# Decoder block with expert mixer: digits in smaller groups, U chunks ahead of the one-hots, the last block's routes earlier, gate stores on ScalarE's queue

## The chip, the cores and the metric

The kernel runs on one core of one Trainium2 chip. The metric is the device time of one execution in microseconds, the median of several runs.

## What is computed

One decoder layer on 512 tokens of width 1024. Two groups of heads (16 state-space heads, 8 latent-attention heads) read one input projection and are mixed by one output projection. The change lies in what comes behind them, a product-key expert mixer (PEER): each token chooses, in each of 8 heads, 16 of 16384 experts.

```python
q = (xb @ w_query).reshape(T, PEER_HEADS, 2, PEER_HALF_DIM)
s = jnp.einsum('thkd,hknd->thkn', q, sub_keys).astype(jnp.float32)
sv, si = lax.top_k(s, K)                                   # K = 16 of 128, twice
cand_s = (sv[:, :, 0, :, None] + sv[:, :, 1, None, :]).reshape(T, PEER_HEADS, K * K)
cand_i = (si[:, :, 0, :, None] * PEER_N_KEYS + si[:, :, 1, None, :]).reshape(T, PEER_HEADS, K * K)
top_s, top_pos = lax.top_k(cand_s, K)
expert_idx = jnp.take_along_axis(cand_i, top_pos, axis=-1)
gate = jax.nn.softmax(top_s, axis=-1)
u = jnp.take(u_table, expert_idx, axis=0)
act = jax.nn.gelu(jnp.einsum('td,thkd->thk', xb, u), approximate=False)
v = jnp.take(v_table, expert_idx, axis=0)
return jnp.einsum('thk,thkd->td', gate * act, v)
```

The two expert tables are 16384 x 1024 float32 each.

## The kernel before

**Two ways through the experts.** Most tokens go densely: the kernel streams both whole tables once, in 128 chunks of 128 experts. A *U chunk* multiplies 128 rows of the first table with 352 tokens and puts GELU of the product into a tile `act` (`u_halves`, `act` at L1260). A *V chunk* multiplies that, weighted with the gates, with 128 rows of the second table into six PSUM accumulators (L1425, L1426, L1429). The tokens of block 3, and 32 tokens of block 2, fetch their experts' rows instead, by an indirect DMA of GpSimd, and VectorE makes the dot products: the *dots* (`ug_dots`, L1071) for the 32, the *gather* (`gather`, L1484 fetch, L1495 and L1511 products) for block 3.

**A weight.** Products keep float32's precision by three matmuls with split operands (L74, L75 with a high part, L76 with a low one). Each 128x1024 weight tile is loaded raw by SP (`wir`, L93), rounded by ScalarE into HI (`wih` or `wihx`, L111), and VectorE subtracts to get LO (`wil`, L121). Three raw and three LO tiles exist; HI runs one tile ahead. All engines, and SP's queue of loads, go through their instructions in the order in which the program issues them.

**The stages around the change.**
1. While the queries are made, `stage1` takes the 16 best scores per half head; after each second one, `sums` adds the two lists into candidates `cand` (on GpSimd), and a second search takes the best 16 of these.
2. `stage2` calls `routes` for three blocks at once (`nb` = 3): softmax of the best scores (difference `dd` L989, exponential on ScalarE L1010, sum L1011), and the arithmetic on VectorE that turns positions into expert numbers (`ijg`). ScalarE copies the indices into half precision (`tif`, L1019).
3. `build_g` makes a dense gate matrix by one-hot matmuls: 48 steps of 8 tokens. For each, VectorE makes one-hots `oj` (L1160) and `gi` (L1163) from *digits* of the expert numbers (`dhi` L1132, `dlo` L1133, `dgl` with gates L1141), PE does 16 small matmuls (L1185), and ScalarE evicts them into a staging tile `stg` (L1187). The digits are made for 32 tokens at a time, just before the first of them is used, and the last group's gate part in two halves. Every fourth step SP stores the tile in two pieces, 128 KB and 1920 KB (L1191, L1192). From step 1 each step also has one of the 32 dots. U half chunks (`step_u`) are put between the steps, paced evenly to 104 half chunks at the end of the 48 steps.
4. The V phase: U and V chunks in turn, one *pair* at a time. Gate tiles `gt` are loaded by SP (`load_g`), VectorE multiplies them with `act` (L1392), ScalarE and VectorE split the product into `Ph` (L1409) and `Pl` (L1417).
5. Beside it, block 3 runs as a generator (`gather`), advanced after each pair by `pump` with a budget of microseconds: `part(0)` does heads 0 to 3 (load of scores from a scratch tensor `s3d` L1456, searches L948 to L957, `routes` with `nb` = 1); then rows are fetched and used, and after every second row the second part, `part(4)`, heads 4 to 7, moves on by one step. Once rows have begun, their number is paced over the rest of the chunks.

Of the kernel before, what the change touches and what calls it, by code (L numbers as in the profile page):

```python
# [13 lines left out]
F16 = mybir.dt.float16  # L14
# [3 lines left out]
AF = mybir.ActivationFunctionType  # L18
# [13 lines left out]
UG = 32  # L32
# [23 lines left out]
def tile_block(ctx: ExitStack, tc: tile.TileContext, I, out):  # L56
# [914 lines left out]
    def stage1(m):  # L971
        yield top16(rt, sc.pop(m)[:, 0:3], 128, TV4[:, :, m], TI4[:, :, m])
        if m % 2:
            CD[m // 2] = rt.tile([128, 3, 88], F32, name="cand", bufs=2)
            sums(G, CD[m // 2], TV4[:, :, m - 1], TV4[:, :, m])
        for h in sorted(CD):
            if 2 * h + 1 < m or m == 15:
                yield top16(rt, CD.pop(h), 88, TS4[:, :, h], PO4[:, :, h])

    def routes(pl, ts, po, ti_, nb, nh, dst, after=lambda i: None, room=None):  # L980
# [5 lines left out]
        sm_ = lambda nm, dt=F32: pl.tile([128, n], dt, name=nm)  # L986
        d = pl.tile([128, nb, nh, 16], F32, name="dd")
# [6 lines left out]
        ab = lambda e: abf[:, :, e]  # L994
        V.tensor_scalar(p3, pos, 3, None, op0=OP.logical_shift_right)
# [14 lines left out]
        A.activation(f4(d), f4(d), AF.Exp)  # L1010
# [6 lines left out]
        for i in sorted(range(nb), key=lambda z: z != 2):  # L1017
            for c in range(2):
                A.activation(ti[:, i, :, :, :, c].rearrange("p e h a -> p h e a"),  # L1019
                             ti_[:, i].rearrange("p (h e) a -> p h e a", e=2), AF.Copy)  # L1020
            eq = room if room is not None else pl.tile(sh, F16, name="eq")
            abv = abf[:, i].rearrange("p e (h k) -> p (e h) k", k=16)
            V.tensor_tensor(eq, abv[:, :, None, :].to_broadcast(sh), IA["t"][:, None].to_broadcast(sh), op=OP.is_equal)
            yield 0.15 + nh * 0.27
            eqv = eq.rearrange("p g a (k c) -> p (g a) k c", c=2)
            tv = ti[:, i].rearrange("p e h a c -> p (e h a) c")
            V.tensor_tensor(eqv, eqv, tv[:, :, None, :].to_broadcast([128, 32 * nh, 8, 2]), op=OP.mult)
            yield 0.15 + nh * 0.27
            for w in (8, 4, 2):
                V.tensor_tensor(eq[:, :, :w], eq[:, :, :w], eq[:, :, w:2 * w], op=OP.add)  # L1030
            e4 = eq.rearrange("p (e h) a k -> p e h a k", e=2)
            V.tensor_tensor(dst(i)[:, 0:2], e4[:, :, :, 0], e4[:, :, :, 1], op=OP.add)
            yield 0.6 + nh * 0.27
            after(i)
# [89 lines left out]
    def digits(b, q0):  # L1124
        jT, gT, dT = GT[b]
        n = 32
        hi = gb.tile([128, n, 16, 2], F16, name="dhi")
        lo = gb.tile([128, n, 8, 2], F16, name="dlo")
        gl = gb.tile([128, n, 2, 8, 2], F16, name="dgl")
        dv = lambda e, w: dT[:, e, q0 * 2:(q0 + n) * 2].rearrange("p (q c) -> p q c", c=2)[:, :, None, :].to_broadcast([128, n, w, 2])  # L1130
        io = lambda w: iotaE[:, None, 0:w, :].to_broadcast([128, n, w, 2])
        V.tensor_tensor(hi, io(16), dv(0, 16), op=OP.is_equal)  # L1132
        V.tensor_tensor(lo, io(8), dv(1, 8), op=OP.is_equal)  # L1133
        DG[0] = hi, lo, gl
        yield 1.2

    def gated(b, q0, s0, s1):
        gT = GT[b][1]
        hi, lo, gl = DG[0]
        n = s1 - s0  # L1140
        V.tensor_tensor(gl[:, s0:s1], lo[:, s0:s1, None].to_broadcast([128, n, 2, 8, 2]),  # L1141
                        gT[:, q0 + s0:q0 + s1, :, None, :].to_broadcast([128, n, 2, 8, 2]), op=OP.mult)

    def build_g():
        def hot(n):
            b, g = divmod(n, 16)
            jT = GT[b][0]
            if g % 8 == 0:
                for _ in digits(b, g * 4):
                    pass  # L1150
            if g % 8 == 0:
                gated(b, g * 4, 0, 16 if n == 40 and UG == 32 else 32)
            if n == 48 - UG // 8 and UG == 32:
                gated(b, 32, 16, 32)
            q0 = g % 8 * 4
            hi, lo, gl = DG[0]
# [11 lines left out]

        nxt = hot(0)
        dots, head = ug_dots(), ug_head()  # L1170
        u0 = un[0] * 2 - (half[0] is not None)
        for n in range(48):
# [16 lines left out]
            if g % 4 == 3:  # L1189
                qv = lambda z: z.rearrange("j (q i) t -> j q (i t)", i=4)  # L1190
                nc.sync.dma_start(gs0[:, :, b * 4 + g // 4].rearrange("q j x -> j q x"), qv(stg[:, 0:8]))  # L1191
                nc.sync.dma_start(gsp[:, :, b * 4 + g // 4].rearrange("q j x -> j q x"), qv(stg[:, 8:]))  # L1192
            if g == 12 and b < 2:
                g_head(b + 1)
            if n >= DOT0:
                next(dots, 0.0)
            if HEAD0 <= n < HEAD0 + 5:
                next(head, 0.0)
            while un[0] * 2 - (half[0] is not None) < u0 + (2 * (LEAD - RES) - u0) * (n + 1) / 48:
                if not step_u(LEAD - RES if len(aps) > 1 else KEEP):  # L1200
                    break
# [164 lines left out]
    def load_g(q):  # L1366
        if q < 32 and q not in gt:
            gt[q] = vst.tile([128, NT // 32, 4, 32], F32, name="gt", bufs=2)
            nc.sync.dma_start(gt[q].rearrange("p b i t -> p (b i t)"),
# [71 lines left out]
    def gather():  # L1441
# [12 lines left out]
        def part(h0):  # L1454
# [6 lines left out]
            yield 0.1  # L1461
            for m in range(0, 8, 2):
# [25 lines left out]
        for s in range(256):  # L1488
# [5 lines left out]
            if s < 128:  # L1494
                V.scalar_tensor_tensor(r, r, 1.0, x3, op0=OP.mult, op1=OP.mult, accum_out=hd[:, s:s + 1])  # L1495
                if other is not None and s % 2:
# [207 lines left out]
```

## Time and profile before

| | |
|---|---|
| median of 3 runs | 1638.58 us (1638.53 to 1643.16) |
| the profiled execution | 1647.61 us |
| its span | 1645.8 us |
| its mean granted PE clock | 0.986 |
| DMA, whole span | 404.41 MB, mean 246 GB/s |

The profile is one execution, with a start, a length and the idle time ahead for each instruction or group of equal ones. In `start us, us, engine line op out<-in [idle before <-releaser]` the bracket is the time that the engine stood before the instruction, and what ended that. Records of one engine overlap a little, so the distance from start to start is what an instruction costs in a row of them. A row by windows gives the busy time of each engine in a stretch, the clock that PE was granted, the share of time in which the 16 DMA engines moved something, and GB/s. PE, PEld, DVE, ACT, POOL and SP are TensorE's matmuls, its weight loads, VectorE, ScalarE, GpSimd and SyncE.

### The profile page before, as it was taken

How to read it: one execution, taken by the hardware profiler on the slowest of the kernel's cores; microseconds unless marked ns; L12 is line 12 of the kernel's file. 1: busy time of each engine (PE TensorE's matmuls, PEld its weight loads, DVE VectorE, ACT ScalarE, POOL GpSimd, SP SyncE). 2: the span in 40 equal slices, each digit the busy share in tenths (PEclk: the TensorE clock that was granted, in tenths of full speed). 3: DMA queues.
4: the chain of work that ended last, by engine and by line, in shares of the span. 5: the costliest groups of instructions: out<-in, count | busy, mean ns of one | idle time of the engine just before them, and what ended most of it. 6: DMA issues, size and time to landing. Idle time of an engine off the chain costs nothing.

```text
span 1645.8 us, 23832 instructions
## 1 busy us (share of the span) xinstructions
PE 1578.0 (96%) x8640; PEld 1385.0 (84%) x8640; DVE 1361.7 (83%) x2684; ACT 692.6 (42%) x1106; POOL 496.3 (30%) x373
## 2 busy tenths in 40 slices
PE   7999989999999989889898989999999999999997
PEld 5778877888888989889887889999999999888886
DVE  8979678847677689988387989888888989999978
ACT  5575456631433445445342233333333333333332
POOL 0000000000144213320003455655555555555400
PEclk9999999999999999999999999999999999999999
DMA  6242121364433459997757889999999999999963
GB/s 242 92 153 90 46 62 47 108 233 141 137 101 99 130 179 328 335 332 238 243 159 275 311 307 395 369 359 371 358 350 380 354 362 361 372 358 336 369 227 118
DMA packets 158459, 404.41 MB, mean 246 GB/s; under 512 B 13100, under 2 KB 67820, under 8 KB 158084
## 3 DMA queue, kind: packets, MB, share of 16 engines
q1 hardware_dynamic: 110644, 238.88, 42.8%
q0 software_dynamic: 45248, 162.68, 26.9%
q8 instruction: 68, 1.11, 0.3%
q10 hardware_dynamic: 2448, 1.31, 0.3%
q14 instruction: 51, 0.42, 0.1%
HBM read 369.19 MB, written 32.59 MB: 244 GB/s over the span
## 4 chain that ended last, share of the span: by engine, by line
PE 77%; DVE 11%; DMA 6%; issue 2%; ACT 2%; POOL 1%; SPq 0%; DVEq 0%; ACTq 0%; POOLq 0%
PE va L1425 9%; PE va L1426 9%; PE va L1429 9%; PE pu L74 8%; PE pu L76 8%; PE pu L75 8%; DMA wir<-ut 3%; PE pw L76 3%; PE pw L75 3%; PE pw L74 3%; PE pa L74 3%; PE pa L76 3%; PE pa L75 3%; DVE wil L121 2%; DMA s<-s3d 1%
## 5 line engine op out<-in xcount | busy, mean ns | idle before, releaser
L111 ACT ACTIVATE wih<-wir 128x1024 fp32r<-128x1024 f32 (+2 forms) x269 | 278.1, 1035 | 293.7 <-DMA wir<-v 119.1
L121 DVE TENSOR_TENSOR wil<-wir,wih 128x1024 fp32r<-128x1024 f32 (+1 forms) x253 | 300.9, 1190 | 76.8 <-ACT wih L111 42.1
L76 PE MATMUL pu<-XTH,wil 128*128 128x352 f32 x1008 | 328.5, 326 | 18.4 <-DVE wil L121 18.4
L74 PE MATMUL pu<-XTH,wih 128*128 128x352 f32 x904 | 297.0, 329 | 0.9 <-ACT act L1260 0.9
L75 PE MATMUL pu<-XTL,wih 128*128 128x352 f32 x904 | 293.1, 324 | 0.0
L1426 PE MATMUL va<-wil,Ph 128*128 128x512 f32 x726 | 282.9, 390 | 0.0
L1484 POOL DMA_INDIRECT row<-u,ix x128 | 184.9, 1444 | 269.1 <-DVE row L1495 126.0
L1484 POOL DMA_INDIRECT row<-v,ix x128 | 189.2, 1478 | 155.6 <-DVE ac L1511 131.5
L76 PEld LDWEIGHTS pu<-XTH,wil 128*128 128x128 f32 x1008 | 192.2, 191 | 20.4 <-DVE wil L121 20.4
L74 PEld LDWEIGHTS pu<-XTH,wih 128*128 128x128 f32 x904 | 171.7, 190 | 4.1 <-ACT act L1260 1.2
L75 PEld LDWEIGHTS pu<-XTL,wih 128*128 128x128 f32 x904 | 171.8, 190 | 2.9
L1425 PE MATMUL va<-wih,Ph 128*128 128x512 f32 x432 | 168.3, 390 | 0.0
L1511 DVE SCALAR_TENSOR_TENSOR ac<-row,hd,ac 128x1024 f32<-128x1024 f32 x128 | 164.1, 1282 | 3.9 <-DMA row<-v,ix 1.7
L1495 DVE SCALAR_TENSOR_TENSOR row<-row,x 128x1024 f32<-128x1024 f32 x128 | 151.9, 1219 | 11.5 <-DMA row<-u,ix 10.2
L1426 PEld LDWEIGHTS va<-wil,Ph 128*128 128x128 f32 x726 | 136.3, 188 | 25.8
L111 ACT ACTIVATE wihx<-wir 128x1024 fp32r<-128x1024 f32 x67 | 71.0, 1060 | 193.4 <-DMA wir<-v 164.4
L1429 PE MATMUL va<-wih,Pl 128*128 128x512 f32 x432 | 133.0, 389 | 0.0
L1260 ACT ACTIVATE act<-pu 128x352 f32<-128x352 f32 x126 | 58.2, 462 | 146.5 <-PE pu L76 142.1
L1425 PE MATMUL va<-wihx,Ph 128*128 128x512 f32 x294 | 114.8, 390 | 0.8 <-ACT Ph L1409 0.8
L121 DVE TENSOR_TENSOR wil<-wir,wihx 128x1024 fp32r<-128x1024 f32 x62 | 75.8, 1222 | 33.9 <-issue 25.1
L1429 PEld LDWEIGHTS va<-wih,Pl 128*128 128x128 f32 x432 | 81.1, 188 | 17.0
L1425 PEld LDWEIGHTS va<-wih,Ph 128*128 128x128 f32 x432 | 81.1, 188 | 15.6
(469 smaller groups left out, 3023.3 us busy)
## 6 DMA issues: line engine op xcount, KB each, us to landing
wir<-ut SPq DMA_DIRECT2D x128, 512.0 KB
wir<-v SPq DMA_DIRECT2D x128, 512.0 KB
gsp<-stg SPq DMA_DIRECT2D x12, 1920.0 KB
gt<-gsp SPq DMA_DIRECT2D x30, 768.0 KB
wir<-wo SPq DMA_DIRECT2D x26, 512.0 KB
wir<-wf SPq DMA_DIRECT2D x18, 512.0 KB
wir<-wqr SPq DMA_DIRECT2D x16, 512.0 KB
de<-acd POOLq DMA_DIRECT2D x8, 512.0 KB
```

The costliest lines, as they stand in the source:

```text
L74: T.matmul(ps, lh, rh, start=start, stop=False)
L75: T.matmul(ps, lh, rl, start=False, stop=False)
L76: T.matmul(ps, ll, rh, start=False, stop=stop)
L111: A.activation(h, r, AF.Copy)
L121: self.lo(n).tensor_tensor(l, r, h, op=OP.subtract)
L1260: A.activation(ACT[c], ps, AF.Gelu)
L1425: T.matmul(va[b][e], Ph[b], h[:, cs], start=c == 0, stop=False)
L1426: T.matmul(va[b][e], Ph[b], l[:, cs], start=False, stop=False)
L1429: T.matmul(va[b][e], Pl[b], h[:, cs], start=False, stop=c == 127)
L1484: G.indirect_dma_start(out=R[s], out_offset=None, in_=I["u"] if s < 128 else I["v"], in_offset=bass.IndirectOffsetOnAxis(ap=ix[:, s % 128: ...
L1495: V.scalar_tensor_tensor(r, r, 1.0, x3, op0=OP.mult, op1=OP.mult, accum_out=hd[:, s:s + 1])
L1511: V.scalar_tensor_tensor(ac, r, hd[:, s - 128:s - 127], ac, op0=OP.mult, op1=OP.add)
```

## The change

It has eight parts.

1. In `stage1`, the last candidate sums (m = 15) move from GpSimd to VectorE.
2. In `routes` for one block (`nb` = 1), the exponential and the two index copies go to ScalarE right behind the difference `dd`, ahead of the position arithmetic. For three blocks nothing moves.
3. Digits are made for 16 tokens at a time, all three parts together, in double buffers, two steps ahead of their use.
4. Two U half chunks go between the first digits and the first one-hots, and one behind these; the pace under the 48 steps is steeper up to step 32 and flatter after.
5. The gate stores are issued by ScalarE.
6. The first two gate loads are issued by GpSimd.
7. Each part of the last block yields 9.0 us of budget between the load of its scores and the first search.
8. `part(4)` starts behind row 10 instead of row 0.

```diff
@@ stage1
-            sums(G, CD[m // 2], TV4[:, :, m - 1], TV4[:, :, m])
+            sums(V if m == 15 else G, CD[m // 2], TV4[:, :, m - 1], TV4[:, :, m])
@@ routes
+        def tis(i):
+            for c in range(2):
+                A.activation(ti[:, i, :, :, :, c].rearrange("p e h a -> p h e a"),
+                             ti_[:, i].rearrange("p (h e) a -> p h e a", e=2), AF.Copy)
...
+        if nb == 1:
+            A.activation(f4(d), f4(d), AF.Exp)
+            tis(0)
         V.tensor_scalar(p3, pos, 3, None, op0=OP.logical_shift_right)
...
-        A.activation(f4(d), f4(d), AF.Exp)
+        if nb > 1:
+            A.activation(f4(d), f4(d), AF.Exp)
...
-            for c in range(2):
-                A.activation(ti[:, i, :, :, :, c].rearrange("p e h a -> p h e a"),
-                             ti_[:, i].rearrange("p (h e) a -> p h e a", e=2), AF.Copy)
+            if nb > 1:
+                tis(i)
@@ digits
-    def digits(b, q0):
+    def digits(n):
+        b, g = divmod(n, 16)
         jT, gT, dT = GT[b]
-        n = 32
-        hi = gb.tile([128, n, 16, 2], F16, name="dhi")
+        q0, w = g * 4, 16
+        hi = gb.tile([128, w, 16, 2], F16, name="dhi", bufs=2)
...
@@ build_g, hot(n)
-            if g % 8 == 0:
-                for _ in digits(b, g * 4):
-                    pass
-            if g % 8 == 0:
-                gated(b, g * 4, 0, 16 if n == 40 and UG == 32 else 32)
-            if n == 48 - UG // 8 and UG == 32:
-                gated(b, 32, 16, 32)
-            q0 = g % 8 * 4
-            hi, lo, gl = DG[0]
+            hi, lo, gl = DG[n // 4 * 4]
+            if n % 4 == 3:
+                DG.pop(n - 3)
+            q0 = g % 4 * 4
@@ build_g
+        digits(0)
+        for _ in range(2):
+            step_u()
         nxt = hot(0)
+        step_u()
...
-                nc.sync.dma_start(gs0[:, :, b * 4 + g // 4].rearrange("q j x -> j q x"), qv(stg[:, 0:8]))
-                nc.sync.dma_start(gsp[:, :, b * 4 + g // 4].rearrange("q j x -> j q x"), qv(stg[:, 8:]))
+                nc.scalar.dma_start(gs0[:, :, b * 4 + g // 4].rearrange("q j x -> j q x"), qv(stg[:, 0:8]))
+                nc.scalar.dma_start(gsp[:, :, b * 4 + g // 4].rearrange("q j x -> j q x"), qv(stg[:, 8:]))
...
+            if n % 4 == 2 and n < 44:
+                digits(n + 2)
...
-            while un[0] * 2 - (half[0] is not None) < u0 + (2 * (LEAD - RES) - u0) * (n + 1) / 48:
+            um = 2 * (KEEP - 1)
+            to = u0 + (um - u0) * (n + 1) / 32 if n < 32 else um + (2 * (LEAD - RES) - um) * (n - 31) / 16
+            while un[0] * 2 - (half[0] is not None) < to:
@@ load_g
-            nc.sync.dma_start(gt[q].rearrange("p b i t -> p (b i t)"),
+            (G if q < 2 else nc.sync).dma_start(gt[q].rearrange("p b i t -> p (b i t)"),
@@ gather, part(h0)
             yield 0.1
+            yield 9.0
             for m in range(0, 8, 2):
@@ gather, rows
-                if other is not None and s % 2:
+                if other is not None and s > 10 and s % 2:
```

The first place is VectorE at the start of the 48 steps. Before, behind the last routes:

```order
L1032 TENSOR_TENSOR ijg<-eq 128x256
L121 TENSOR_TENSOR wil<-wir,wih 128x1024
L1132 TENSOR_TENSOR dhi<-iotaE,dT 128x1024
L1133 TENSOR_TENSOR dlo<-iotaE,dT 128x512
L1141 TENSOR_TENSOR dgl<-dlo,gT 128x1024
L1160 TENSOR_TENSOR oj<-iotaE,jT 128x1024
L1163 TENSOR_TENSOR gi<-dhi,dgl 128x2048
L1160 TENSOR_TENSOR oj<-iotaE,jT 128x1024
L1163 TENSOR_TENSOR gi<-dhi,dgl 128x2048
L121 TENSOR_TENSOR wil<-wir,wih 128x1024
```

And now, the same engine and place:

```order
L1041 TENSOR_TENSOR ijg<-eq 128x256
L121 TENSOR_TENSOR wil<-wir,wih 128x1024
L1142 TENSOR_TENSOR dhi<-iotaE,dT 128x512
L1143 TENSOR_TENSOR dlo<-iotaE,dT 128x256
L1144 TENSOR_TENSOR dgl<-dlo,gT 128x512
L121 TENSOR_TENSOR wil<-wir,wih 128x1024
L1159 TENSOR_TENSOR oj<-iotaE,jT 128x1024
L1162 TENSOR_TENSOR gi<-dhi,dgl 128x2048
L121 TENSOR_TENSOR wil<-wir,wih 128x1024
L1159 TENSOR_TENSOR oj<-iotaE,jT 128x1024
L1162 TENSOR_TENSOR gi<-dhi,dgl 128x2048
```

The digits have half the elements, and a LO subtraction for a U half chunk stands before each of the first two pairs of one-hots, where both pairs stood together.

The second place is the stores. Before, on SP, between the loads of weights:

```order
L93 DMA wir<-ut 128x1024 x14
L1191 DMA gs_69<-stg 128x2x128
L1192 DMA gsp<-stg 128x30x128
L93 DMA wir<-ut 128x1024 x2
L1191 DMA gs_69<-stg 128x2x128
L1192 DMA gsp<-stg 128x30x128
```

Now they stand on ScalarE, between evictions and HI copies:

```order
L1267 ACTIVATE act<-pu 128x352
L1190 ACTIVATE stg<-pw 128x128x4 x2
L1194 DMA gs_69<-stg 128x2x128
L1195 DMA gsp<-stg 128x30x128
L111 ACTIVATE wih<-wir 128x1024
```

SP has nothing left but loads there, and ScalarE issues each pair of stores right behind the eviction that fills the tile.

The third place is VectorE where the second part of the last block's routes begins beside the gathered rows. Before:

```order
L121 TENSOR_TENSOR wil<-wir,wih 128x1024
L1495 SCALAR_TENSOR_TENSOR row,hd<-row,x_8496 128x1024 x2
L948 MAX tv_9078<-s_9076 128x8 x2
L950 MAX_INDEX ti_9079<-tv_9078,s_9076 128x8 x2
L953 MATCH_REPLACE t_9154<-tv_9078,s_9076 128x128
```

Now:

```order
L121 TENSOR_TENSOR wil<-wir,wih 128x1024
L1503 SCALAR_TENSOR_TENSOR row,hd<-row,x_8531 128x1024 x4
L121 TENSOR_TENSOR wil<-wir,wih 128x1024
L1424 TENSOR_TENSOR Pl<-gt,Ph 128x384
L1399 TENSOR_TENSOR gt<-act,gt 128x11x32
L121 TENSOR_TENSOR wil<-wir,wihx 128x1024
L1503 SCALAR_TENSOR_TENSOR row,hd<-row,x_8531 128x1024
L948 MAX tv_9581<-s_9579 128x8 x2
L950 MAX_INDEX ti_9582<-tv_9581,s_9579 128x8 x2
```

The first search (MAX) of the second part comes behind 16 rows of the gather now, where it came behind four.

More of the change, by code (lines that the diff above doesn't have):

```diff
@@ L1122, in tile_block @@
     DG = {}
-    def digits(b, q0):
+    def digits(n):
+        b, g = divmod(n, 16)
         jT, gT, dT = GT[b]
-        n = 32
-        hi = gb.tile([128, n, 16, 2], F16, name="dhi")
[L1128 to L1131, printed above, removed]
+        q0, w = g * 4, 16
+        hi = gb.tile([128, w, 16, 2], F16, name="dhi", bufs=2)
+        lo = gb.tile([128, w, 8, 2], F16, name="dlo", bufs=2)
+        gl = gb.tile([128, w, 2, 8, 2], F16, name="dgl", bufs=2)
+        dv = lambda e, k: dT[:, e, q0 * 2:(q0 + w) * 2].rearrange("p (q c) -> p q c", c=2)[:, :, None, :].to_broadcast([128, w, k, 2])
+        io = lambda k: iotaE[:, None, 0:k, :].to_broadcast([128, w, k, 2])
         V.tensor_tensor(hi, io(16), dv(0, 16), op=OP.is_equal)
         V.tensor_tensor(lo, io(8), dv(1, 8), op=OP.is_equal)
[L1134 to L1138, printed above, removed]
-        hi, lo, gl = DG[0]
-        n = s1 - s0
-        V.tensor_tensor(gl[:, s0:s1], lo[:, s0:s1, None].to_broadcast([128, n, 2, 8, 2]),
-                        gT[:, q0 + s0:q0 + s1, :, None, :].to_broadcast([128, n, 2, 8, 2]), op=OP.mult)
+        V.tensor_tensor(gl, lo[:, :, None].to_broadcast([128, w, 2, 8, 2]),
+                        gT[:, q0:q0 + w, :, None, :].to_broadcast([128, w, 2, 8, 2]), op=OP.mult)
+        DG[n] = hi, lo, gl
     def build_g():
@@ L1147, in hot @@
             jT = GT[b][0]
-            if g % 8 == 0:
-                for _ in digits(b, g * 4):
-                    pass
-            if g % 8 == 0:
-                gated(b, g * 4, 0, 16 if n == 40 and UG == 32 else 32)
-            if n == 48 - UG // 8 and UG == 32:
-                gated(b, 32, 16, 32)
-            q0 = g % 8 * 4
-            hi, lo, gl = DG[0]
+            hi, lo, gl = DG[n // 4 * 4]
+            if n % 4 == 3:
+                DG.pop(n - 3)
+            q0 = g % 4 * 4
             oj = gb.tile([128, 4, 128, 2], F16, name="oj", bufs=2)
```

## The prediction

> **What bounds the kernel now.** I read the page first. TensorE (PE) sets the time.
>
> ```profile
> PE 1578.0 (96%) x8640; PEld 1385.0 (84%) x8640; DVE 1361.7 (83%) x2684; ACT 692.6 (42%) x1106; POOL 496.3 (30%) x373
> ```
>
> A change can win only where PE stands still or runs at a low clock, so the waits of PE come next, then the busy times by stretch: one row for the 48 steps of one-hots and dots, one for their middle, one for the start of the V phase, one for the last block's second half of scores and routes, one for the steady pairs of a U and a V chunk, and one for 20 of those.
>
> ```profile
> PE pu L76 <- DVE wil L121: 18.4, 7, 6.9
> PE pw L1185 <- DVE gi L1163: 13.9, 8, 4.3
> ```
>
> ```profile
> 603.35:741.60 138.25, 127.54 (x1095) 121.89 (x1093) 128.44 (x172) 68.97 (x124) 41.12 (x29) 0.97 0.94 313
> 620.00:720.00 100.00, 91.94 (x815) 87.50 (x813) 95.06 (x127) 49.70 (x87) 36.10 (x25) 1.00 1.01 342
> 820.00:840.00 20.00, 14.61 (x70) 13.68 (x71) 18.22 (x73) 5.51 (x8) 0.00 (x0) 0.83 0.54 171
> 878.65:975.91 97.26, 85.79 (x425) 76.66 (x424) 84.64 (x220) 32.49 (x45) 40.31 (x30) 0.95 0.83 295
> 960.00:1300.00 340.00, 339.08 (x1786) 309.01 (x1787) 302.75 (x419) 125.06 (x171) 193.86 (x133) 0.99 0.97 362
> 980.00:1000.00 20.00, 20.00 (x110) 18.32 (x109) 18.61 (x29) 5.77 (x8) 12.88 (x9) 1.00 0.99 388
> ```
>
> The columns are stretch, length, busy PE, PEld, DVE (VectorE), ACT (ScalarE), POOL (GpSimd), granted clock, DMA share and GB/s. In the steady pairs PE is busy 339.08 of 340 us: nothing is to be had there. In the dots VectorE is the fuller engine (128.44 against 127.54), in their middle clearly (95.06 against 91.94), with the DMA engines at 1.01. At the start of the V phase PE is busy 14.61 of 20 at clock 0.83, with VectorE at 18.22. In the second half of the routes PE has 85.79 of 97.26. Call these places A, B and C; the change works on all three.
>
> **A: one-hots and dots.** Before the 48 steps VectorE makes digits for 32 tokens and two one-hots, and PE waits for them.
>
> ```profile
> 601.75 1.86 PE L1185 MATMUL pw<-gi,oj 128*128 128x128 f16 x16 [4.30 <-DVE gi L1163]
> ...
> 609.06 0.32 PE L76 MATMUL pu<-XTH,wil 128*128 128x352 f32 x1
> 609.22 1.10 PE L1185 MATMUL pw<-gi,oj 128*128 128x128 f16 x16
> ```
>
> ```profile
> 598.21 0.68 DVE L1132 TENSOR_TENSOR dhi<-iotaE,dT 128x1024 f16<-128x1024 f16 x1
> 598.81 0.42 DVE L1133 TENSOR_TENSOR dlo<-iotaE,dT 128x512 f16<-128x512 f16 x1
> 599.26 0.69 DVE L1141 TENSOR_TENSOR dgl<-dlo,gT 128x1024 f16<-128x1024 f16 x1
> 599.87 0.69 DVE L1160 TENSOR_TENSOR oj<-iotaE,jT 128x1024 f16<-128x1024 f16 x1
> 600.48 1.22 DVE L1163 TENSOR_TENSOR gi<-dhi,dgl 128x2048 f16<-128x2048 f16 x1
> 601.61 0.69 DVE L1160 TENSOR_TENSOR oj<-iotaE,jT 128x1024 f16<-128x1024 f16 x1
> 602.21 1.22 DVE L1163 TENSOR_TENSOR gi<-dhi,dgl 128x2048 f16<-128x2048 f16 x1
> 603.35 1.22 DVE L121 TENSOR_TENSOR wil<-wir,wih 128x1024 fp32r<-128x1024 f32 x1
> ```
>
> After the wait the same 16 matmuls take 1.86 us instead of 1.10, so the gap costs a slow clock as well. By the starts, digits for 32 tokens take 1.66 us (598.21 to 599.87), an oj 0.61, a gi 1.13 (600.48 to 601.61). The changed kernel has half-size digits; between half and all of 1.66 I estimate 1.1. It puts three U half chunks on PE before the first one-hot matmuls. A half chunk is 12 matmuls, and one starts 0.16 us after the other (609.06 to 609.22), so it takes 1.92 us. Three are 5.76 us, more than the 4.30 that PE waits. The order puts two LO subtractions between the digits and the second pair of one-hots, each at the 1.13 of a gi, whose record is as long; VectorE then starts its steady part at 598.21 + 1.1 + 2 x 1.13 + 2 x 1.74 = 605.05, against 603.35. From there to 741.6 it has 128.44 us of work and 9.8 idle. After: one LO fewer (-1.1), eight digit groups of 1.1 instead of four of 1.66 (+2.2): 129.6. With half of the idle time kept, 4.5, it ends at 739.2, 2.4 earlier, and one whole U chunk (3.84 us of PE) further. **A = -6.2.** Bounds: if all idle time stays, 605.05 + 129.6 + 9.8 = 744.5, which with the chunk gives -1; if none stays, 734.7 and -10.8. "U thicker" is hardly done under the dots themselves: by the order a step there has 1.41 half chunks, and 1.42 before; what counts is the three ahead.
>
> The last candidate sums on VectorE end this wait, the earlier start is 10.8 us less about 0.5 for three sums:
>
> ```profile
> 549.12 0.56 DVE L948 MAX8 ts<-cand 128x8 f32<-128x88 f32 x3 [10.80 <-POOL cand L965]
> ...
> 563.29 0.55 DVE L1011 TENSOR_REDUCE smm<-dd 128x24 f32<-128x384 f32 x1 [3.69 <-ACT dd L1010]
> ```
>
> I cost it at nothing. The exponential of that stage (three blocks, not moved by the change) keeps its place in ScalarE's row behind the U evictions that PE paces, and VectorE already waits 3.69 us for it at 563.29: what it gains at 549 it waits there. If that is wrong, up to 10 us more are to be had, which would show as VectorE reaching the digits before 590.
>
> The stores by ScalarE: SP issued one in 0.46 us, so 24 of them put some 11 us on ScalarE, which has 69 us of idle time in 138.25. The cover is that idle time; what is gained is that the next weight loads do not queue behind a store that waits for its staging tile.
>
> ```profile
> 632.77 0.46 SPq L1192 DMA_DIRECT2D gsp<-stg  x1
> 636.36 6.11 SPq L93 DMA_DIRECT2D wir<-ut  x1
> ```
>
> That gain lies in the 5 us of idle that I take off A. The two first gate loads by GpSimd no longer stand behind SP's loads of weights. VectorE waited for them here:
>
> ```profile
> 804.71 0.53 DVE L1392 TENSOR_TENSOR gt<-act,gt 128x352 f32<-128x352 f32 x1 [6.01 <-DMA gt<-gs]
> ```
>
> PE still had U chunks to do, so I give it 0, between -1 and +1.
>
> **B: start of the V phase.** The load of the last block's scores was issued at 812.02, and VectorE, its next user in order, stood 8.76 us until 819.43; everything behind it, the LO of the next weights too, was late, and PE waited 6.93 us for that.
>
> ```profile
> 819.43 0.49 DVE L948 MAX8 tv<-s 128x8 f32<-128x128 f32 x2 [8.76 <-DMA s<-s3d]
> ```
>
> ```profile
> 812.02 0.43 SPq L1456 DMA_DIRECT2D s<-s3d  x1
> ```
>
> ```profile
> 825.39 0.66 PE L76 MATMUL pu<-XTH,wil 128*128 128x352 f32 x1 [6.93 <-DVE wil L121]
> ```
>
> ```profile
> 814.08 0.46 ACT L1260 ACTIVATE act<-pu 128x352 f32<-128x352 f32 x1
> ...
> 831.05 0.47 ACT L1260 ACTIVATE act<-pu 128x352 f32<-128x352 f32 x1
> ...
> 838.99 0.47 ACT L1260 ACTIVATE act<-pu 128x352 f32<-128x352 f32 x1 [2.73 <-PE pu L76]
> ```
>
> From eviction to eviction an undisturbed pair takes 7.94 us (831.05 to 838.99); the two from 814.08 to 838.99 took 24.91, so 9.0 were lost. The change lets the first search start two V chunks, some 16 us, after the load: twice the 7.4 that it took to land. Next late would be the search work itself, and VectorE's two LO tiles of lead cover a burst. **B = -9**, bounds -7 (its work shows at one pair) and -9.8 (with the clock kept up).
>
> **C: second half of the routes beside the gather.**
>
> ```profile
> L1260 ACT ACTIVATE act<-pu x11: 438/446/465, 878.7 to 975.9; 128x352 f32<-128x352 f32 x11
> ```
>
> Eleven evictions, so ten pairs, in 97.26 us: 17.9 over ten of 7.94. VectorE's row says of what: its 84.64 busy is 5.2 over 79.4, and 12.6 was idle. Most of that idle is two waits:
>
> ```profile
> 889.38 0.49 DVE L948 MAX8 tv<-s 128x8 f32<-128x128 f32 x2 [5.09 <-DMA s<-s3d]
> ...
> 955.61 0.22 DVE L1011 TENSOR_REDUCE smm<-dd 128x4 f32<-128x64 f32 x1 [5.19 <-ACT dd L1010]
> ```
>
> ```profile
> 952.54 1.06 ACT L111 ACTIVATE wih<-wir 128x1024 fp32r<-128x1024 f32 x1 [4.26 <-DMA wir<-ut]
> ```
>
> The exponential stood behind a HI copy that waited 4.26 us for its weights. After: the score load goes out four rows (more than a pair) before its use, and the exponential goes to ScalarE some ten VectorE operations and two rows earlier. The idle time goes, the 5.2 of work stays. **C = -12.6**; bounds -7.7 (only the two waits go, 10.3, and 2.6 come back as weights that are late) and -17.9 (the lead hides the work too).
>
> **Steady pairs.** By the order the gather starts three V chunks later and ends at the same chunk: 256 rows over some 79 pairs instead of 82, 3.24 a pair for 3.12, 0.06 MB on 2.87 (two weight loads, 3.12 rows of 0.524 MB, a quarter of a 768 KB gate load): 370 GB/s where 362 ran. The 388 at 980 passed with PE busy all 20 us. I take +1, bounds 0 and +6.
>
> **Sum:** -6.2 - 9 - 12.6 + 1 = -26.8 against the profiled execution's 1647.61, so 1620.8; that one lay 9.03 over the median of three, 1638.58, and I take the same difference off it: **1611.8**.
>
> **Rivals.** *The DMA engines set the pace.* Where PE falls behind they are at 1.01 with 342 GB/s, and a store issued by another engine moves the same bytes. Then A is only what leaves the full stretch early, three half chunks or 0.79 MB at 342 GB/s, -2.3; B and C stay (C's 28.7 MB at 362 GB/s fit in 79.3 us); and if 362 GB/s is the most that the steady mix gets, 2.2% of 79 pairs of 7.94 us come on top, +13.8. Sum -10, 1628. For it: the share of 0.97. Against: 388 GB/s at 980. The Trainium skill (DMA: Bandwidth & Descriptors, "Issuing engines are not separate DMA queues") says that transfers started by different engines run on the same 16 DMA engines and save only issue time, and its section "Where 436 GB/s comes from" puts a core's HBM at about 358 GB/s, which would give this rival's time; the trace's 362 over 340 us is near that figure and its 388 over 20 us above it, so the row decides for now.
>
> *Stores hold ScalarE up; slower.* Its row is in order: HI copies, evictions and GELU stand behind a store that takes long to issue. A single issue behind such a store took 6.11 us on SP. With HI one chunk ahead, 3.84 us are hidden; 12 times (6.11 - 3.84) is +27.2, which cancels all the gain: about 1639. At 8 us an issue it is +50, so 1662. It decides from 6.1 us an issue. Against it: SP's own 0.46 for the store itself.
>
> *All waits go:* A -10.8, B -9.8, C -17.9, together -38.5: 1600.
>
> **How the numbers follow.** Forecast 0.55, DMA pace 0.25, all waits 0.08, ScalarE held up 0.12 (a part of it small, 0.02 still faster, 0.05 at no change, 0.05 slower). The forecast's own range, is 1604 to 1620: the bounds lie some 5, 1.5, 5 and 3 us from the terms of A, B, C and the steady pairs, and errors of their own are together about 8. To hold 8 in 10 it must reach into the DMA case and the full gain: 1600 to 1631. About 0.3%, 4.9 us, is what a measurement of this kernel can tell from no change; the DMA case has a tenth of its chance there. Faster 0.55 + 0.22 + 0.08 + 0.02 = 0.87, same 0.08, slower 0.05.
>
> **What would show it.** Right: no wait of PE for gi over 1 us before the first one-hot matmuls; no wait of VectorE over 2 us for the scores at either search; evictions 7.94 us apart through the first ten pairs; the dots ending some 2 us earlier. Wrong: steady pairs over 8.0 us with the DMA share at 1 (the DMA rival); waits on ScalarE or of VectorE for wih behind each store (the ScalarE rival); VectorE's waits moved to weights instead of gone.

## The result

The changed kernel takes 1628.37 us (median of 4 runs, 1626.13 to 1628.64); the kernel before takes 1640.3 beside it and 1641.64 over 29 runs of the experiments' first series. The ratio to before is 0.9923, 95% interval 0.9903 to 0.9942: about 12 to 13 us faster, where 26.8 were forecast. The time lies in the range given, 16.6 us above the forecast of 1611.8.

The first two rows of the page after, and PE's longest waits:

```profile
span 1624.4 us, 23835 instructions
...
PE 1571.6 (97%) x8640; PEld 1379.0 (85%) x8640; DVE 1364.0 (84%) x2704; ACT 693.5 (43%) x1106; POOL 513.8 (32%) x372
```

```profile
PE pa L287 <- ACT XH L282: 11.5, 2, 10.9
PE pw L1188 <- DVE gi L1162: 8.2, 7, 2.1
PE pu L76 <- DVE wil L121: 7.6, 5, 4.2
```

PE's wait for LO fell from 18.4 to 7.6 us, that for the one-hots from 13.9 to 8.2. The wait for XH lies in the first stage, which the change does not touch.

Profile against profile the gain is 21.4 us (1645.8 to 1624.4), median against median 12 to 13. To see where both numbers come from I cut each trace at five instructions: the first eviction of a U chunk, the last one-hot matmul (`pw<-gi,oj`), and three of the low-part products of the V chunks (`va` from `Pl`, six a chunk): the first, the 49th (ninth chunk) and the 169th (twenty-ninth chunk). Starts are taken from the trace, differences in us. An undisturbed pair takes 7.93 us, so eight of them are 63.5 and twenty 158.7. What lies ahead of the first U eviction is left out of the table: no edit stands there, and it took from 529.9 to 533.2 us in these traces (533.2 in the first profile of before, 531.3 in the changed kernel).

| kernel | first U to last one-hot | to the first V product | 8 V chunks (B) | next 20 (C) | to the end |
|---|---|---|---|---|---|
| before, first profile | 258.2 | 15.5 | 72.5 | 175.7 | 590.7 |
| before, second profile | 258.3 | 15.3 | 72.2 | 169.2 | 590.7 |
| changed | 250.9 | 16.8 | 63.5 | 171.0 | 590.8 |
| only one-hots | 248.8 | 15.3 | 73.5 | 172.8 | 590.8 |
| only queues | 255.3 | 16.1 | 72.0 | 173.7 | 590.8 |
| only first gap | 257.5 | 15.4 | 63.5 | 170.4 | 590.8 |
| only second part | 256.8 | 15.4 | 72.3 | 167.9 | 590.7 |
| three ahead | 255.0 | 15.4 | 73.9 | 172.7 | 590.8 |
| all but queues | 251.7 | 15.6 | 63.5 | 171.1 | 590.7 |
| all but exponential | 251.0 | 16.3 | 63.5 | 171.8 | 591.1 |
| all, scores earlier | 249.9 | 16.4 | 63.5 | 167.1 | 590.8 |
| all, spread | 250.1 | 16.4 | 63.5 | 162.0 | 590.8 |
| all, rows thin | 250.0 | 16.4 | 63.5 | 160.0 | 610.1 |
| gap and spread | 257.6 | 15.6 | 63.5 | 163.4 | 590.7 |

Three columns decide. A (the first two) and B changed as forecast; C hardly changed, and C is also the only stretch of the table that two executions of one and the same program do not repeat (175.7 and 169.2).

Now the places. At the first one-hots of the changed kernel PE goes from a U matmul straight into the 16 small ones (the row holds the first 14 of them):

```profile
601.00 0.32 PE L76 MATMUL pu<-XTH,wil 128*128 128x352 f32 x1
601.17 0.99 PE L1188 MATMUL pw<-gi,oj 128*128 128x128 f16 x14
```

The windows of the changed kernel, in the columns of the prediction: the steps that have a dot, the first eight V chunks, the twenty behind them, a stretch at the second part's first search, and the steady pairs.

```profile
603.00:740.00 137.00, 128.50 (x1109) 122.31 (x1108) 133.65 (x191) 71.33 (x123) 40.09 (x30) 0.98 0.97 326
799.00:862.50 63.50, 63.50 (x338) 57.75 (x337) 45.60 (x151) 28.61 (x41) 0.00 (x0) 1.00 0.57 184
862.50:1033.50 171.00, 163.26 (x842) 146.88 (x841) 150.60 (x319) 59.81 (x83) 83.38 (x60) 0.98 0.88 318
930.00:950.00 20.00, 16.19 (x73) 15.15 (x74) 20.00 (x69) 5.66 (x9) 7.63 (x7) 0.83 0.76 257
1055.00:1380.00 325.00, 325.00 (x1722) 295.63 (x1721) 292.94 (x361) 120.41 (x166) 191.55 (x133) 1.00 0.99 375
```

The first eight V chunks are without a gap (63.50 of 63.50). In the steps with dots VectorE is at 133.65 of 137. (The prediction calls its row to 741.60 that of all 48 steps; the one-hot matmuls go on, to 791.4 before and 782.2 now.) At 930 the picture of the old B is back: PE at 16.19 of 20 and clock 0.83, VectorE full. What begins there, in the order VectorE, SP, PE:

```profile
925.57 0.49 DVE L948 MAX8 tv<-s 128x8 f32<-128x128 f32 x2 [4.02 <-DMA s<-s3d]
```

```profile
911.05 0.85 SPq L1463 DMA_DIRECT2D s<-s3d  x1
```

```profile
933.81 0.66 PE L76 MATMUL pu<-XTH,wil 128*128 128x352 f32 x1 [4.21 <-DVE wil L121]
```

The load of the scores was issued at 911.05 and used at 925.57: 14.5 us, beside the gather's rows, where the same size of load at the start of the V phase before had taken 7.4. The kernel before has a load at this place too, the one that VectorE waits for at 889.38. Both score loads stand in its chain of work (start, us, what):

```profile
812.02 7.29 DMA s<-s3d
...
872.41 16.95 DMA s<-s3d
```

So 17 us for this load stood in the trace from which the prediction was made.

### The profile page after: what moved, and what is told of

The parts are those of the page before. It is cut to its first block, busy times and chain, and to the rows that moved or that the text cites. A ratio compares the mean times of both kernels' runs of the same rounds, so it can differ in the third digit from the quotient of the medians.

```text
span 1624.4 us, 23835 instructions
## 1 busy us (share of the span) xinstructions
PE 1571.6 (97%) x8640; PEld 1379.0 (85%) x8640; DVE 1364.0 (84%) x2704; ACT 693.5 (43%) x1106; POOL 513.8 (32%) x372
## 4 chain that ended last, share of the span: by engine, by line
PE 78%; DVE 14%; DMA 4%; ACT 2%; issue 2%; DVEq 0%; SPq 0%; ACTq 0%
PE va L1432 9%; PE va L1433 9%; PE va L1436 9%; PE pu L74 8%; PE pu L76 8%; PE pu L75 8%; PE pw L75 3%; PE pw L76 3%; PE pw L74 3%; PE pa L74 3%; PE pa L76 3%; PE pa L75 3%; DVE wil L121 3%; DVE row L1503 2%; PE pw L1188 2%
## 5 line engine op out<-in xcount | busy, mean ns | idle before, releaser
L1492 POOL DMA_INDIRECT row<-v,ix x128 | 205.6, 1606 | 127.7 <-DVE ac L1519 101.0
L121 DVE TENSOR_TENSOR wil<-wir,wihx 128x1024 fp32r<-128x1024 f32 x62 | 75.7, 1221 | 26.8 <-issue 14.2
L121 POOL TENSOR_TENSOR wil<-wir,wih 128x1024 fp32r<-128x1024 f32 x16 | 38.4, 2400 | 178.5 <-PE pw L76 171.9
```

Of the source, the lines that this page charges most:

```text
L121: self.lo(n).tensor_tensor(l, r, h, op=OP.subtract)
L1492: G.indirect_dma_start(out=R[s], out_offset=None, in_=I["u"] if s < 128 else I["v"], in_offset=bass.IndirectOffsetOnAxis(ap=ix[:, s % 128: ...
```

## The experiments

Ratios are to the kernel before, with 95% intervals. First the parts alone, on the kernel before.

**Only the one-hots** (parts 1, 3 and 4 of the change).

```diff
+            sums(V if m == 15 else G, CD[m // 2], TV4[:, :, m - 1], TV4[:, :, m])
+        q0, w = g * 4, 16
+        digits(0)
+        for _ in range(2):
+            step_u()
         nxt = hot(0)
+        step_u()
+            if n % 4 == 2 and n < 44:
+                digits(n + 2)
```

> The kernel before with only the smaller digit groups, the three U half chunks ahead of the one-hots, the pace and the sums on VectorE (parts 1, 3, 4). Theory (each part pays for itself where it stands; the PE wait at the first one-hots goes): the wait of 4.3 us of PE for gi goes and V0 comes 4 to 6 us earlier, median -4 to -6. Rival (the stores out of SP's queue are what frees the 48 steps): this alone gives -2 or less, and weight loads still come late behind the stores.

Measured: 1634.18, ratio 0.9958 (0.9944 to 0.9972), -7 us. The stretch to the first V product fell from 273.7 to 264.1. The theory holds, with more than it asked for; B and C are not touched.

**Only the queues** (parts 5 and 6).

```diff
-                nc.sync.dma_start(gs0[...], ...)
-                nc.sync.dma_start(gsp[...], ...)
+                nc.scalar.dma_start(gs0[...], ...)
+                nc.scalar.dma_start(gsp[...], ...)
-            nc.sync.dma_start(gt[q]...
+            (G if q < 2 else nc.sync).dma_start(gt[q]...
```

> The kernel before with only the gate stores issued by ScalarE and the two first gate loads by GpSimd (parts 5, 6). Theory: 0, between -2 and +2. Rival (the queue frees the 48 steps): -3 to -6 in the 48 steps. Rival (ScalarE is held up by issues): slower by 3 or more, with idle time on ScalarE behind each store.

Measured: 1640.77, ratio 0.9996 (0.9984 to 1.0008): nothing, in neither direction. In the changed kernel's trace a pair of stores costs ScalarE about 1 us, all 24 stores 10.8 us. The first pair:

```profile
615.55 0.38 ACTq L1194 DMA_DIRECT2D gs<-stg  x1
615.96 0.59 ACTq L1195 DMA_DIRECT2D gsp<-stg  x1
616.65 1.06 ACT L111 ACTIVATE wih<-wir 128x1024 fp32r<-128x1024 f32 x1 [1.13 <-DVE urow L1080]
```

The rival that ScalarE is held up is out: the issues take 0.37 to 0.73 us, not 6. The table shows a small loss and a small gain that cancel: with the gate loads on GpSimd the second column is 16.1 to 16.8 us, in all other kernels 15.3 to 15.6, and the first column of this kernel is 1.4 to 2.9 us shorter than in the kernels with the old one-hots and the stores on SP.

**Only the first gap** (part 7, for the first four heads alone).

```diff
             yield 0.1
+            if not h0:
+                yield 9.0
```

> The kernel before with only the 9.0 us of budget between the load of the first four heads' scores and their first search. Theory: the 8.8 us wait of VectorE and the 6.9 us wait of PE go, -7 to -9 in the profile at the start of the V phase, and the median follows with -6 to -9 if the median execution of before has that loss too. Rival (the profiled execution of before lost more there than a typical one): the profile gains 9, the median 4 or less. Rival (the DMA engines set the pace, so what is won is lost later): profile of the end -3 or less.

Measured: 1630.28, ratio 0.9932 (0.991 to 0.9953), -11 us. B is 63.5, exactly eight undisturbed pairs, 9 us less; the rest is in C (170.4) and in differences between executions. One line has nearly the whole gain of the change.

**Only the second part** (parts 2 and 8, and 7 for the last four heads).

```diff
+        if nb == 1:
+            A.activation(f4(d), f4(d), AF.Exp)
+            tis(0)
+            if h0:
+                yield 9.0
-                if other is not None and s % 2:
+                if other is not None and s > 10 and s % 2:
```

> The kernel before with only the second part: exponential and index copies ahead of the position arithmetic, start behind row 10, one more step between load and search (parts 2 and 8, and 7 for the second part). Theory (the searches and the score load are only moved, the wait for the exponential goes): -3 to -5. Prediction's own figure: -12.6. Rival (all of it is given back as VectorE work in a bunch): 0.

Measured: 1636.23, ratio 0.9971 (0.9955 to 0.9986), -5 us. C fell to 167.9, so 9.2 us over twenty free pairs: the theory's size, not the prediction's 12.6.

The four parts alone add up to about -24 us, the change gives -13. The missing part is not in B. In A the one-hots alone reached 264.1 and the changed kernel 267.7; in C the first gap alone has 170.4, the second part alone 167.9, and both together, with the rest, 171.0. So the next kernels start from the changed one, and first ask how much of C was there to be had.

**Before once more**, for a second profile; no line is edited.

> The kernel before once more, for a second profile. Theory (the first profiled execution of before was an unlucky one): the stretch from the first U eviction to the first V product (273.7 us in the first profile) and that from the ninth V chunk to the twenty-ninth (175.6) come out 1 to 3 us shorter each, the start of the V phase again at 72.5. Rival (the profile itself costs what the medians do not show): the same 273.7 and 175.6 within 0.5.

Measured: 1639.06, and C took 169.2 where it had taken 175.7; A did not get shorter (273.6 in all), so the theory is right for one stretch of the two. The same two waits of VectorE in the second profile of before:

```profile
884.32 0.49 DVE L948 MAX8 tv<-s 128x8 f32<-128x128 f32 x2 [4.14 <-DMA s<-s3d]
...
947.79 0.22 DVE L1011 TENSOR_REDUCE smm<-dd 128x4 f32<-128x64 f32 x1 [2.42 <-ACT dd L1010]
```

They had been 5.09 and 5.19. Five traces have the second part of before unchanged, behind a gather that also starts as before: the two of before, only the one-hots, only the queues, and three ahead (below). Their C is 175.7, 169.2, 172.8, 173.7 and 172.7, on average 172.8, against 171.0 and 171.1 in the two that have the whole second part as changed (the changed kernel, and all but the queues). **The change is worth some 1.8 us in C on average**, with 6.5 us between executions of one program: against the second profile of before C became 1.8 longer, so even the sign is not shown.

**All but the queues**: the changed kernel with the stores and gate loads on SP again.

```diff
-                nc.scalar.dma_start(gs0[...], ...)
+                nc.sync.dma_start(gs0[...], ...)
...
-            (G if q < 2 else nc.sync).dma_start(gt[q]...
+            nc.sync.dma_start(gt[q]...
```

> The changed kernel with its stores and first gate loads back on SP. Theory (stores in ScalarE's row and the gate loads by GpSimd take 3.6 us back from the one-hots' gain, 267.7 against 264.1 in the stretch to the first V product): that stretch returns to 264 to 265, median 2 to 4 below the changed kernel. Rival (they are worth nothing either way): within 1.

Measured: 1627.57, ratio 0.9915 (0.9902 to 0.9928), against 0.9923 (0.9903 to 0.9942) of the changed kernel: the same. The stretch to the first V product is 267.3, so the 3.6 us between 264.1 and 267.7 are not the queues'. My theory falls. Up to the first V product this kernel and the one-hots alone are the same program, and yet they differ by 3.2 us; the one-hots' 264.1 may have been a good execution.

**All but the exponential**: the exponential and index copies of the last block behind the arithmetic again.

```diff
-        if nb == 1:
-            A.activation(f4(d), f4(d), AF.Exp)
-            tis(0)
...
-        if nb > 1:
-            A.activation(f4(d), f4(d), AF.Exp)
+        A.activation(f4(d), f4(d), AF.Exp)
```

> The changed kernel with the exponential and the index copies of the last block back behind the position arithmetic. Prediction's step: the wait of 5.2 us for the exponential comes back, +5. Rival (ahead of the arithmetic the exponential waits for VectorE in ScalarE's row and holds the next HI copy up, so it only changes the place of the wait): 0, within 1.5.

Measured: 1626.4, ratio 0.9908 (0.9893 to 0.9922): no difference; C is 171.8 against 171.0. The rival holds. Ahead of the arithmetic the exponential waits in ScalarE's row for VectorE, in the changed kernel:

```profile
968.33 0.26 ACT L1002 ACTIVATE dd<-dd 128x64 f32<-128x64 f32 x1 [2.81 <-DVE dd L995]
```

The edit is worth nothing here because the wait that it removes is not there by then: without it, in this kernel, the sum behind the exponential has no wait in the last block (and 0.4 us in the kernel before with gap and spread, below).

**All, with the scores earlier**: three more steps, six rows, between load and search.

```diff
             yield 9.0
+            for _ in range(3 if h0 else 0):
+                yield 0.1
```

> The changed kernel with three more steps (six rows) between the load of the last four heads' scores and their first search. Theory (what is left in the second part is the late score transfer): VectorE's 4.0 us wait and PE's 4.2 us wait behind it go, and the 12.4 us lost from the ninth to the twenty-ninth V chunk become about 6: -5 to -6. Rival (the work of the second part is itself more than VectorE has room for): the wait goes, the loss stays at 10 or more, -2 or less.

Measured: 1623.45, ratio 0.9897 (0.988 to 0.9914), 4 to 5 us less than the changed kernel, with intervals that overlap. The search does not wait any more, C is 167.1 (171.0 to 171.8 in three traces without this edit). So the late score transfer is worth some 4 of the 12.3 us that C has over free pairs, and 8.4 are left. What they are, in a stretch of this run:

```profile
943.00:975.00 32.00, 26.52 (x135) 22.92 (x133) 32.00 (x107) 10.01 (x13) 13.72 (x11) 1.00 0.86 301
```

VectorE is busy 32.00 of 32 without a wait, PE 26.52, the clock is full and the DMA engines are not (0.86). Both theories were half right: the wait has its price, and what is left is larger. That it is VectorE's own work in a bunch is the reading that the next kernel tests.

**All, spread**: the second part moves on at every third row from row 6.

```diff
-                if other is not None and s > 10 and s % 2:
+                if other is not None and s > 4 and s % 3 == 0:
```

> The changed kernel with the second part moved on at every third row from row 6 instead of every second from row 11: the same work over 51 rows instead of 34, six rows between score load and first search. Theory (what is left in the second part is VectorE's own work in a bunch: 14 us beside ten pairs that leave room for 9): over 16 pairs the room is 14, so the loss from the ninth to the twenty-ninth V chunk, 12.4 in the changed kernel and 8.5 with only the scores earlier, falls to 0 to 4; median 8 to 12 below the changed kernel, VectorE not full. Rival (the weights come late there because the DMA engines are full): the loss stays near 8.5.

Measured: 1617.88, ratio 0.9859 (0.984 to 0.9878), 10.5 us less than the changed kernel: the forecast of the theory in full. C is 162.0, 3.3 over free pairs. The whole stretch of the changed kernel stands above as the row from 862.50; here it is with the same work spread:

```profile
860.00:1022.10 162.10, 159.34 (x842) 144.35 (x842) 149.88 (x319) 59.67 (x83) 82.60 (x59) 1.00 0.91 335
```

VectorE has 149.88 us of work, and had 150.60; only its place is another. The stretch is 8.9 us shorter, at a higher rate of the DMA engines (335 GB/s for 318), so these did not limit it.

**All, rows thin**: fewer rows a pair beside the second part, more behind it.

```diff
             want = 253 - max(0.0, 256 * (left - ENDU) / GS[1])
+            if w == 2.0:
+                cap += 2.4 if GS[0] < 56 else 3.6
+                want = min(want, cap)
```

> The changed kernel with at most 2.4 rows a pair up to row 56 and 3.6 after it, until the U chunks end. Theory (VectorE's bunch): the loss from the ninth to the twenty-ninth V chunk falls from 12.4 to 2 to 5, and the rest of the kernel behind the twenty-ninth, 590.8 us in all runs so far, grows by 0 to 5 as its pairs carry more rows. Rival (DMA engines at their limit in the steady pairs): at 3.6 rows a pair of 7.93 us they would have to move 395 GB/s, and the rest grows by 10 or more.

Measured: 1633.62, ratio 0.9945 (0.9925 to 0.9965). C fell to 160.0, as VectorE's theory has it (though fewer rows also take DMA traffic out of C); but the rest of the kernel, 590.7 to 591.1 in all others, took 610.1. The steady pairs of before, in their first profile, and of this kernel:

```profile
1055.00:1380.00 325.00, 325.00 (x1722) 295.72 (x1722) 286.89 (x358) 120.61 (x166) 180.71 (x127) 1.00 0.97 362
```

```profile
1055.00:1380.00 325.00, 316.30 (x1653) 283.44 (x1652) 291.49 (x369) 112.22 (x155) 196.17 (x139) 1.00 0.98 368
```

At 3.6 rows a pair the demand would be 395 GB/s (3.6 rows of 0.524 MB and 1.25 MB of weights and gates in 7.93 us); 368 came, and PE stood. VectorE, at 291.49 of 325, was not full. That fits the rival, but it does not show a ceiling at 368, nor at the changed kernel's 375 (share 0.99, PE busy all 325 us), for the kernel before moved more in its steady pairs without a gap on PE:

```profile
987.50:1028.60 41.10, 41.10 (x221) 37.52 (x220) 38.05 (x58) 16.01 (x22) 24.40 (x18) 1.00 1.01 395
```

From the twenty-ninth V chunk on PE's waits in the thin kernel are nearly all for VectorE's LO (10.0 us in 12 waits; the changed kernel has none), and VectorE stood 27.0 us for gathered rows there (17.9 in the changed kernel). So rows that land late may be part of it; what makes up the 19.3 us stays open, for no run separates the causes.

**Three ahead**: the kernel before with three U half chunks ahead of the first digits, nothing else.

```diff
+        for _ in range(3):
+            step_u()
         nxt = hot(0)
```

> The kernel before with three U half chunks ahead of the first digits and one-hots and nothing else of the change. Theory (the half chunks ahead are what the first stage wins by): PE's 4.3 us wait goes, the 272 to 273 us to the first V product become 266 to 268, median -4 to -6. Rival (smaller digit groups and their place two steps ahead, in the 48 steps, are what wins): 0 to -2.

Measured: 1639.15, ratio 0.9979 (0.9966 to 0.9992), -2 to -3 us. The stretch to the first V product is 270.4, in neither range: between the 266 to 268 of the theory and the 272 to 273 of the rival. The wait at the first one-hot matmuls became shorter but did not go (the row holds 15 of the 16):

```profile
604.89 1.41 PE L1187 MATMUL pw<-gi,oj 128*128 128x128 f16 x15 [2.85 <-DVE gi L1163]
```

```profile
601.35 0.68 DVE L1132 TENSOR_TENSOR dhi<-iotaE,dT 128x1024 f16<-128x1024 f16 x1
```

VectorE makes the LO of the half chunks ahead of the digits here, so the digits begin 69.3 us behind the first U eviction, where they began 65.0 behind it before, and also in the changed kernel, which makes its first digits ahead of the half chunks. So the half chunks alone bring about half of A's gain. The rest comes with digits, pace and sums together; no run separates these. (A group of digits serves eight steps before and four now, 64 and 32 tokens: the 32 and 16 of the description and the code count pairs of tokens.)

**Gap and spread**: the kernel before with two lines.

```diff
             yield 0.1
+            yield 9.0
...
-                if other is not None and s % 2:
+                if other is not None and s > 4 and s % 3 == 0:
```

> The kernel before with two lines only: the 9.0 us of budget behind the score loads, and the second part at every third row from row 6. None of the one-hots, queues or exponential parts. Theory (two separate losses, each gone by its own edit): 63.5 us for the first eight V chunks and 162 to 165 for the next twenty, so some 9 + 8 to 11 below a typical execution of before, about 1622; the stretch to the first V product stays at 272 to 273. Rival (the exponential ahead and the one-hots carry part of the gain in the V phase): the twenty pairs take 167 or more, about 1627.

Measured: 1622.0, ratio 0.9876 (0.9853 to 0.9899). B is 63.5, C 163.4, A as before at 273.2. The theory's 1622 holds: B and C are two separate losses. B is gone, and one line does it (only first gap); C is down to 4.7 over free pairs by the two lines together, for the 9.0 us also stand between the second load of scores and its search. The kernel beats the changed one by 6 us; with the other parts as well (all, spread) the median is 1617.88, the lowest of all kernels here, though the two intervals overlap.

## Why the prediction was wrong

**A, -6.2: right**, to 0.2 us with some luck. 273.7 became 267.7, -6.0. PE's wait at the first one-hots is gone, and the first 14 matmuls behind it take 0.99 us, so the slow clock is gone too. The parts are others than in the sum: the last dot starts 199.4 us behind the first U eviction, where it started 204.4 behind it, so 5.0 earlier for a forecast 2.4, with PE 0.7 of a U chunk further for a forecast one; then 1.3 us are lost again in the table's second column, where VectorE stands 7.31 us ahead of the first gate product for 6.01 before. That VectorE's earlier start in the routes of three blocks is worth nothing is right too: it waits for the exponential there 3.58 us, as it had 3.69, and the digits begin 65.0 us behind the first U eviction in both.

```profile
561.42 0.56 DVE L1021 TENSOR_REDUCE smm<-dd 128x24 f32<-128x384 f32 x1 [3.58 <-ACT dd L1020]
```

**Stores and gate loads, 0: right** for both together, shown from both sides by two runs; the stores took ScalarE 10.8 us, where 11 were reckoned.

**B, -9: right** to the tenth: 72.5 to 63.5, and one line alone does it. This loss repeats: 72.0 to 73.9 in all six traces without the line.

**C, -12.6: wrong; this is the term that failed**, and it failed twice.

1. *The step "The score load goes out four rows (more than a pair) before its use ... The idle time goes, the 5.2 of work stays".* The transfer took 14.5 us there, not the 7.4 that I had read at the start of the V phase, where the DMA engines had room (share 0.72, in the last section). I took the figure from the wrong one of two loads: at 872.41 the trace of before has 17 us for the very load that I moved, so a lead of a little over a pair could not hide it. The 4.0 us wait stayed, with PE's 4.2 us and a clock of 0.83 behind it. And the work was mis-sized. I set 5.2 us as an average over ten pairs, some of them light; that VectorE cannot lend their spare time over more than its two tiles of lead is argued, not shown. What is shown is that with the wait for the scores gone 8.4 us stay (scores earlier) and that spread over 51 rows the same work costs 3.3.
2. *The base.* The 17.9 us came from one execution. Five traces of the unchanged second part have 10.5, 14.0, 14.1, 15.0 and 17.0 us over twenty free pairs, and mine was the worst of them. Against my own profile C gained 4.7, against the average of the five 1.8. The wait for the exponential, 5.2 us, was 2.4 in the second profile; it hangs on when ScalarE gets there, behind a HI copy that waits for its weight. Its edit is worth nothing in the changed kernel.

**The sum's last step, "I take the same difference off it": wrong.** It assumed that the 9 us by which the profiled execution lay over the median were spread over what the change does not touch. Of the 8.5 us between the two profiles of before, 6.5 lie in C, 3.7 of them in the two waits whose end I counted as gain. A loss that the median run does not have cannot be won there. In numbers: the two profiled executions differ by 21.5 us (A 6.0, B 9.0, C 4.7, and 1.9 ahead of the first U eviction, where no edit stands). The one of before lay 7.3 over its median of 1640.3 and the one of the changed kernel 2.2 under its own, and without these 9.5 the medians' 12 are left.

**Steady pairs, +1: 0 to a tenth** (590.7 and 590.8), with 375 GB/s for 362.

**The rivals.** The DMA case gave 1628, and 1628.4 was measured, but not by its mechanism: A won its 6 us, not 2.3, and the steady pairs paid nothing where it had them pay 13.8. Its limit of 362 GB/s does not hold: the changed kernel moves 375 over 325 us and the kernel before 395 over 41.1 us, both without a gap on PE. The Trainium skill (DMA: Bandwidth & Descriptors, "Where 436 GB/s comes from") puts the limit of a core's HBM at about 358, half of a stack's 716 for its two cores; this kernel runs on one core, and its trace is above that figure. Nor does 358 give this rival's time, though the prediction says so: by the prediction's own 370 GB/s it would cost some 21 us (an estimate) in the steady pairs, not 13.8. What the Trainium skill says of issuing engines (DMA: Bandwidth & Descriptors, "Issuing engines are not separate DMA queues": they share the same 16 DMA engines) fits: to move the stores and two gate loads to other engines' queues gave a ratio of 0.9996.

**Open:** why the parts alone add up to more than the whole, in A (3.6 us) and in C, where the second part alone leaves 9.2 us and the whole 12.3. Single profiles of C differ by up to 6.5 us for one and the same code, and of A by 3.2, so these differences may not be ones of the kernels.

## What to carry to other kernels

A stall read from one profile is a sample: before a gain is built on it, look at the same stretch in a second execution, and never take the difference between a profile and the median as something that stays. A transfer is issued ahead by the time that it takes in the traffic at that place, not by that of a quiet one. Where an engine that feeds the bottleneck is full for some tens of us and has room around that, spread its work over more steps: with the scores there in time, the same 150 us of VectorE's work cost 8.4 us at a step every second row and 3.3 at every third.

## What the runs showed of the hardware

A 512 KB load of scores landed in 7.4 us at the start of the V phase before, where the DMA engines had room, in 17.0 us beside the gather of the same kernel, and in 14.5 us beside that of the changed kernel, where they had none. The rows are those times as windows, two of the kernel before and one of the changed one (share and GB/s stand last):

```profile
812.00:819.40 7.40, 6.46 (x33) 5.45 (x31) 0.00 (x0) 2.58 (x3) 0.00 (x0) 1.00 0.72 228
```

```profile
872.40:889.40 17.00, 17.00 (x91) 15.37 (x90) 8.13 (x13) 3.15 (x5) 7.28 (x7) 1.00 1.01 367
```

```profile
911.00:925.60 14.60, 14.60 (x80) 13.41 (x79) 8.67 (x15) 3.18 (x5) 6.16 (x5) 1.00 1.03 383
```

In the steady mix of weights, gathered rows and gates the DMA engines moved 375 GB/s over 325 us, and 395 over 41.1 us, while PE had no gap. A store that ScalarE issues costs its row 0.37 to 0.73 us (24 stores).
